# Hybrid decoder layer on one core: convolution taps tied to the weight splits and spread over more panels, block copies shared by two engines, and a reordered last norm

## The chip, the core and the metric

The kernel runs on one core of a Trainium2 chip. Four engines matter here: TensorE (PE, the matmuls; PEld is its weight load), VectorE (DVE), ScalarE (ACT) and GpSimd (POOL); SyncE (SP) issues the DMAs. The metric is the device time of one execution in microseconds, as the median of several runs.

## The reference

One layer, float32, for 256 tokens (x) and 256 memory tokens (mem), both 4096 wide:

```
proj = x @ w_in[l]                                  # 4096 x 11280
(c_a, c_b, c_gate, g_q, g_k, g_v, g_lr, g_gate, m_q, m_gate) = split(proj)
y_conv = _conv_group(c_a, c_b, dw, dw_b, ln_g, ln_b) * silu(c_gate)   # c_a * sigmoid(c_b), 31 taps per channel, norm, silu
y_gla  = _gla_group(g_q, g_k, g_v, g_lr, ...) * silu(g_gate)          # gated linear attention in chunks of 64
y_mem  = _memory_group(m_q, mem @ w_mem_kv[l]) * silu(m_gate)         # 4 heads of attention into the memory
out = concatenate([y_conv, y_gla, y_mem]) @ w_out[l]
x = _layernorm(DN_ALPHA * x + out, ln_g[l], ln_b[l])
```

## The kernel before

**Products.** Each float32 operand is split in two: ScalarE casts it to a rounded `hi` (L122), VectorE subtracts to get `lo` (L123), both in the helper `halves`. A product is then three matmuls, hi by hi, hi by lo and lo by hi. Weights are the moving side (128x512), x the stationary one. The work runs panel by panel (512 output columns) in the order of `STEPS`. A weight chunk is loaded by SP into one of three `raww` buffers; its halves go to four `hiw` and four `low` buffers (`WBUFS`), so the splitting can run ahead of PE by a few tiles and no more.

**Pairs.** Most panels are done two at a time in `pair` (sixteen chunks of 256 rows by 1024 columns). A chunk takes either eight block products (24 matmuls, two weight tiles "b" and "a") or seven (21 matmuls, four weight tiles "c", "a", "y" and "x"). For the seven, VectorE first makes sums of weight blocks: `tx` (L439) and `ty` in two steps (L445, L448), which ScalarE and VectorE then split like weights. The x side needs sums too (`sums`, tiles r, f, eh, el). `BY7` holds for each pair the pattern of eights and sevens, the x units whose chunks go by seven, the units whose sums are made before it, and those freed behind it. `X_AT` says at which chunk of the first pair each x unit is loaded.

**The order of stages.** Pair cb0 (columns c_b and c_a, first half), pair cb1 (second half), `memory` (mem by w_mem_kv, 64 tiles), pair mq, panels q0 and q1, pair k, panels v0 to v4, pairs gg0, gg2 and cg, panels mg0 and mg1, then the output projection: pairs o0, o1, o2 and two single panels.

**Work beside the matmuls.** Everything else (gates, attention, convolution, norms) is queued as closures and issued in between by the `use` function of each tile: `later` (end of a pair), `work` (in portions), and `fill` (convolution taps). A tap (L828, L837) is one VectorE operation on 128 channels; there are 31 for each of eight channel blocks, 248 in all, four blocks behind cb0 and four behind cb1. `FILLS` and `MEM_FILLS` say how many are taken from `fill` at a time. `queue_transpose` turns a 128x1024 tile: one VectorE transposition of 32x32 blocks (L229), then sixteen copies of 32x256 blocks on ScalarE (L243), four to each call of `moves`. It is used 22 times.

**Who sets the order.** The order on each engine is fixed when the program is built: a scheduler takes the instructions of the closures and arranges them, and may pull one ahead of others on its engine. `tc.issue_after(i)` keeps what stands under it behind instruction i. Each engine's queue is the order that the sections below print.

**The end.** The last panel (block 7) is finished token half by token half (tt 0, then tt 1). `norm_stats` makes mean and factor of a half, with a power on GpSimd (L1208); `norm_rows` brings the factors into a row layout by PE; `norm_apply` finishes the other blocks, on VectorE (L1264) or, with `on_pool`, on ScalarE (L1260, L1261) and GpSimd (L1262).

Of the kernel before, what the change touches and what calls it, by code (L numbers as in the profile page):

```python
# [9 lines left out]
F32 = mybir.dt.float32  # L10
# [18 lines left out]
EARLY = 5  # L29
AHEAD = 3  # L30

X_AT = {0: (1,), 1: (2,), 3: (3,), 4: (6,), 5: (4,), 6: (7,), 7: (5,)}

C_A, C_B, C_G, G_Q, G_K, G_V, G_LR, G_G, M_Q, M_G = 0, 1024, 2048, 3072, 4096, 5120, 7168, 7184, 9232, 10256

# [13 lines left out]

BY7 = {  # L50
    ("cb", 0): ("8888888887878787", (6, 7), (), ()),
    ("cb", 1): ("8888878787878787", (5, 6, 7), (5,), (5,)),
    ("mq", 0): ("8888888887878787", (6, 7), (), (6, 7)),
    ("k", 0): ("8888878787878787", (5, 6, 7), (5, 6, 7), (5,)),
    ("gg", 0): ("8888878787878787", (5, 6, 7), (5,), ()),
    ("gg", 2): ("8888878787878787", (5, 6, 7), (), (5,)),
    ("cg", 0): ("8887888788878887", (6, 7), (), (6, 7)),
}

FILLS = {("cb", 1): 1}  # L60
MEM_FILLS = 5


@with_exitstack
def layer_kernel(ctx, tc, xT, memT, xres, w_mem, w_in, w_pairs, w_last, cst, w_gate,
# [54 lines left out]
    def halves(src, hi, lo):  # L120

        nc.scalar.copy(out=hi, in_=src)  # L122
        nc.vector.tensor_tensor(out=lo, in0=src, in1=hi.bitcast(F32), op=ALU.subtract)  # L123

    def w_raw(shape, name):
        serial[0] += 1
# [94 lines left out]
    def queue_transpose(src, dst, then, back=False):  # L221


        st = {}

        def blocks():
            t = tmp.tile([P, 1024], F32, tag="T", name=f"T_{serial[0]}", bufs=1)
            serial[0] += 1
            nc.vector.transpose(out=t, in_=src.rearrange("p a b -> p (a b)"))  # L229
            give(src)  # L230
            st["t"] = t

        def moves(b):
            if b == 0:
                st["d"] = dst()
            tok = "p t (q j c) -> p t q j c"
            feat = "p q (t i c) -> p t q i c"
            flat = "p (q t i c) -> p t q i c" if back else "p (t q j c) -> p t q j c"
            sizes = dict(q=4, t=2, c=32)
            frm = st["t"].rearrange(flat, **sizes)  # L240
            to = st["d"].rearrange(tok if back else feat, c=32, **({"q": 4} if back else {"t": 2}))
            for a in range(4):
                nc.scalar.copy(  # L243
                    out=to[32 * b : 32 * b + 32, :, :, a, :],
                    in_=frm[32 * a : 32 * a + 32, :, :, b, :],
                )

        work.append(blocks)
        for b in range(4):
            work.append(lambda b=b: moves(b))  # L250
        work.append(lambda: then(st["d"]))
# [43 lines left out]
    def flush():  # L295
        while stream:
            stream.popleft()()


    def panel(chunks, width, stat, then, fills=0, apart=0, soon=KT // 2):  # L300

        banks = []
        held = {}
        raw = {}

        def mms(c, tt, w, second):
            for k in range(2):
                kt = 2 * c + k  # L310
                sh, sl = stat(kt // 4)
                for s in (sh,) if second else (sh, sl):
                    nc.tensor.matmul(  # L313
                        banks[tt][:, :width],
                        lhsT=s[:, kt % 4, tt * P : (tt + 1) * P],
                        rhs=w[:, k, :],
                        start=kt == 0 and not second and s is sh,
                        stop=kt == KT - 1 and second,
                    )

        def make(c):
            if c % 2 == 0:
                raw[0] = w_raw([P, 4, width], "w")
                nc.sync.dma_start(
                    out=raw[0], in_=chunks[c // 2].rearrange("p (k n) -> p k n", k=4)
                )
            w = w_tiles([P, 2, width], "w", KT // 2 - apart <= c < KT // 2 - WBUFS)
            halves(raw[0][:, 2 * (c % 2) : 2 * (c % 2) + 2, :], *w)
            held[c] = w

        def use(c):
            if c == 0:
                for tt in range(2):
                    serial[0] += 1
                    banks.append(acc.tile([P, 512], F32, tag="acc", name=f"acc_{serial[0]}"))
            if c < KT // 2 - apart:
                for w in held[c]:
                    for tt in range(2):
                        mms(c, tt, w, w is held[c][1])
            if later:  # L340
                later.popleft()()
            do_work(-(-len(work) // max(1, soon - c)))
            for _ in range(min(fills, len(fill))):
                fill.popleft()()

        for c in range(KT // 2):
            push(lambda c=c: make(c), lambda c=c: use(c))
        after(lambda: then(banks))

        def rest(k, tt):  # L350
            c = KT // 2 - apart + k
            for w in held[c]:
                mms(c, tt, w, w is held[c][1])

        return rest
# [13 lines left out]
    def pair(chunks, order, stat, ext, then, soon=KT // 2, fills=0, units=False, beside=None):  # L369
# [41 lines left out]
        def make(n, i):  # L411
            c, by7, tiles = plan[n]
            if i == 0:
                raw = w_raw([P, 4, 512], "w")
                ap = chunks[c].rearrange("p (k n) -> p k n", k=4)
                if beside and n == 0:

                    x0 = unit_tiles("x")
                    hi, lo = w_tiles([P, 2, 512], "w")
                    for k in range(2):  # L420
                        load(x0, four(xT[0]), k, k + 1)
                        load((raw[:, 2:4, :], hi, lo), ap[:, 2:4, :], 1 - k, 2 - k)
                    st[n, "b"] = hi, lo
                    nc.sync.dma_start(out=raw[:, 0:2, :], in_=ap[:, 0:2, :])
                    x_units[0] = load(x0, four(xT[0]), 2, 4)
                    give(x0[0])
                else:
                    nc.sync.dma_start(out=raw, in_=ap)
                if beside:
                    beside(n)  # L430
                src = st[n] = dict(a=raw[:, 0:2, :], b=raw[:, 2:4, :], c=raw[:, 2:3, :])
                if by7:
                    serial[0] += 1
                    if units:
# [13 lines left out]
                    nc.vector.tensor_tensor(  # L448
                        out=y[:, 1, :], in0=raw[:, 1, :], in1=y[:, 0, :], op=ALU.subtract
                    )  # L450
                    src.update(x=x, y=y)
            nm = tiles[i][0]
            if (n, nm) in st:
                return
            w = tuple(t[:, : 1 if nm == "c" else 2, :] for t in w_tiles([P, 2, 512], "w"))
            halves(st[n][nm], *w)
            st[n, nm] = w
            if i == len(tiles) - 1:
                src = st.pop(n)
                if by7 and units:  # L460
                    give(src["x"], src["y"])

        def use(n, i):
# [10 lines left out]
            for second in range(2):  # L474
                for j, (slot, stationary, bk) in enumerate(terms):
                    sh, sl = stationary(c)
                    for s in (sh,) if second else (sh, sl):
# [4 lines left out]
                            start=first[bk] == (n, nm, j) and not second and s is sh,  # L482
                            stop=last[bk] == (n, nm, j) and second == 1,
                        )
            if later:
                later.popleft()()
            if i == len(tiles) - 1:
                for _ in range(min(fills, len(fill))):
                    fill.popleft()()
                do_work(-(-len(work) // max(1, soon - n)))  # L490

        for n, (_, _, tiles) in enumerate(plan):
            for i in range(len(tiles)):
# [542 lines left out]
    def memory():  # L1036
        m_units, raws, tiles, banks = [], {}, {}, []

        def make(kt, half):
# [6 lines left out]
            if half == 1 and kt % 4 == 1 and kt < KT - 4:  # L1046
                m_units.append(load_unit("mem", four(memT[kt // 4 + 1])))
            tiles[kt, half] = w_tiles([P, 1024], "wm")
            halves(raw, *tiles[kt, half])

        def use(kt, half):
            while later and half == 1:
# [20 lines left out]
                            )  # L1073
            if half and kt % 4 == 3:
                give(mh, ml)
            if later:
                later.popleft()()
            do_work(-(-len(work) // max(1, KT - kt)))
            for _ in range(min(MEM_FILLS, len(fill))):
                fill.popleft()()  # L1080

        def done():
            mk.extend(unit([P, 2, 512], F32, "mk") for _ in range(2))
# [106 lines left out]
    z = []  # L1190
# [10 lines left out]
    def norm_stats(tt, g, beta):  # L1201
# [9 lines left out]
        nc.vector.tensor_scalar(  # L1211
            out=mn, in0=m[:, 0:1], scalar1=-1.0, scalar2=None, op0=ALU.mult
        )
        y = z[7][:, tt, :]
        nc.vector.scalar_tensor_tensor(
            out=y, in0=y, scalar=m[:, 0:1], in1=g, op0=ALU.subtract, op1=ALU.mult
        )
        c = cc[tt]
        nc.vector.tensor_scalar(
            out=c[:, 0:65:64], in0=mn.to_broadcast([P, 2]), scalar1=r, scalar2=None, op0=ALU.mult  # L1220
# [6 lines left out]
            op0=ALU.mult,  # L1227
            op1=ALU.subtract,
        )
        with tc.issue_after(cl.ins):  # L1230
            nc.vector.scalar_tensor_tensor(
                out=y, in0=y, scalar=r, in1=beta, op0=ALU.mult, op1=ALU.add
            )
# [165 lines left out]
    with tc.issue_after(last.ins):  # L1399
# [5 lines left out]
        with tc.issue_after(pw.ins):  # L1405
            norm_apply(0, (6,), on_pool=True)
        norm_rows(1)
        norm_apply(1, range(7))


def make_consts(nc, cpool, cst, norm_g):
# [91 lines left out]
```

## Time and profile before

| | |
|---|---|
| median of 3 runs | 1538.81 us (1537.97 to 1539.09) |
| profiled execution, its own time | 1540.91 us |
| its span in the profile | 1538.9 us |
| PE busy | 1506.4 us, 98%, 6809 matmuls |
| DVE busy | 1210.9 us, 79% |
| ACT busy | 901.6 us, 59% |
| POOL busy | 49.2 us, 3% |
| mean granted clock of TensorE | 0.993 of full speed |

The span runs from the first to the last instruction; the profiled execution's own time is 2.0 us longer, and 2.1 us above the median. A busy PE is not yet a PE at its peak, so how much a stage lost is told by its matmuls' count against its length. The page names the engine that ended each idle time.

### The profile page before, as it was taken

The numbers are of one execution on the slowest core, as the hardware profiler recorded it, in microseconds if no ns is written. First come the engines' busy times: TensorE is split into PE (matmuls) and PEld (weight loads), VectorE is DVE, ScalarE is ACT, GpSimd is POOL, SyncE is SP. The second block draws the span as 40 slices with busy tenths as digits, with TensorE's granted clock in tenths as the row PEclk, the third lists the DMA queues.
The fourth block names the chain that finished last, engine by engine and source line by source line (L and its number), as shares of the span: only waits on it lengthen the run. The fifth ranks groups of instructions, "written<-read, shape, count | busy, mean of one in ns | idle before, by whom it ended". The sixth has DMA issues, their size and how long they took to land.

```text
span 1538.9 us, 18500 instructions
## 1 busy us (share of the span) xinstructions
PE 1506.4 (98%) x6809; PEld 1265.8 (82%) x6809; DVE 1210.9 (79%) x1454; ACT 901.6 (59%) x1203; POOL 49.2 (3%) x59
## 2 busy tenths in 40 slices
PE   8999899999999999999999999999999999999997
PEld 6787678888888888899999887888888887888885
DVE  7799999997686579957575788887757589998955
ACT  6565357438668855676464468577685454555541
POOL 0000000000000000003030000000000000000001
PEclk9999999999999999999999999999999999999998
DMA  8564557765555465555445454656567545565662
GB/s 326 204 219 154 182 172 252 244 206 213 207 189 179 144 238 187 201 197 176 161 156 198 174 213 164 219 218 233 212 219 274 205 178 205 209 216 203 225 223 109
DMA packets 54515, 311.73 MB, mean 203 GB/s; under 512 B 6100, under 2 KB 6484, under 8 KB 27928
## 3 DMA queue, kind: packets, MB, share of 16 engines
q1 hardware_dynamic: 54424, 310.55, 57.1%
q8 instruction: 53, 0.87, 0.2%
q14 instruction: 38, 0.31, 0.1%
HBM read 304.24 MB, written 6.29 MB: 202 GB/s over the span
## 4 chain that ended last, share of the span: by engine, by line
PE 86%; DVE 6%; ACT 3%; issue 3%; DMA 2%; POOL 0%; SPq 0%; DVEq 0%; ACTq 0%
PE acc L478 29%; PE acc L313 28%; PE sm L478 8%; PE acc_N L478 8%; PE mv L1067 6%; PE mk L1067 6%; DVE low L123 2%; DVE cacc L837 2%; ACT S L243 1%; DMA rawx<-xT 1%; DMA raww<-w_in 1%; ACT hiw L122 1%; ACT qkT L243 1%; PE A L749 1%; PE o L274 1%
## 5 line engine op out<-in xcount | busy, mean ns | idle before, releaser
L123 DVE TENSOR_TENSOR low<-raww,hiw 128x1024 fp32r<-128x1024 f32 (+3 forms) x497 | 560.2, 1144 | 171.4 <-ACT hiw L122 139.6
L122 ACT CAST hiw<-raww 128x1024 fp32r<-128x1024 f32 (+3 forms) x497 | 476.7, 978 | 312.9 <-PE acc L313 125.6
L478 PE MATMUL acc<-hiw,hx 128*128 128x512 f32 x528 | 207.7, 393 | 6.1 <-ACT hiw L122 6.1
L313 PE MATMUL acc<-hiw,hx 128*128 128x512 f32 (+2 forms) x576 | 211.8, 368 | 0.1
L313 PE MATMUL acc<-hiw,lx 128*128 128x512 f32 (+2 forms) x576 | 211.7, 368 | 0.0
L478 PE MATMUL acc<-hiw,lx 128*128 128x512 f32 x528 | 206.7, 392 | 0.0
L478 PE MATMUL acc<-low,hx 128*128 128x512 f32 x528 | 169.0, 391 | 6.6 <-DVE low L123 6.6
L313 PE MATMUL acc<-low,hx 128*128 128x512 f32 (+2 forms) x576 | 141.7, 366 | 0.0
L122 ACT CAST hiw<-ty 128x1024 fp32r<-128x1024 f32 x52 | 54.6, 1050 | 130.4 <-DVE ty L448 93.0
L478 PEld LDWEIGHTS acc<-hiw,hx 128*128 128x128 f32 x528 | 100.0, 189 | 29.0 <-ACT hiw L122 8.2
L478 PEld LDWEIGHTS acc<-low,hx 128*128 128x128 f32 x528 | 99.1, 188 | 29.6 <-DVE low L123 9.3
L313 PEld LDWEIGHTS acc<-hiw,hx 128*128 128x128 f32 x576 | 108.2, 188 | 10.9 <-ACT hiw L122 0.4
L478 PEld LDWEIGHTS acc<-hiw,lx 128*128 128x128 f32 x528 | 100.0, 189 | 20.7
L313 PEld LDWEIGHTS acc<-hiw,lx 128*128 128x128 f32 x576 | 108.2, 188 | 10.3
L313 PEld LDWEIGHTS acc<-low,hx 128*128 128x128 f32 x576 | 107.2, 188 | 10.7
L122 ACT CAST hiwm<-rawwm 128x1024 fp32r<-128x1024 f32 x64 | 66.4, 1053 | 73.3 <-PE mv L1067 26.5
L837 DVE SCALAR_TENSOR_TENSOR cacc<-hT,cst_sb,cacc 128x255 f32<-128x255 f32 (+29 forms) x240 | 99.1, 462 | 0.0
L243 ACT COPY S<-T 32x256 f32<-32x256 f32 x224 | 90.3, 403 | 7.0 <-DVE T L229 3.2
L478 PE MATMUL acc<-hiw,xh 128*128 128x512 f32 x224 | 87.4, 390 | 1.6 <-ACT hiw L122 1.6
L123 DVE TENSOR_TENSOR low<-ty,hiw 128x1024 fp32r<-128x1024 f32 x52 | 63.6, 1222 | 31.7 <-ACT hiw L122 21.0
L478 PE MATMUL acc<-hiw,xl 128*128 128x512 f32 x224 | 87.2, 389 | 0.0
L439 DVE TENSOR_TENSOR tx<-raww 128x1024 f32<-128x1024 f32 x52 | 63.4, 1220 | 21.9 <-DMA raww<-w_in 21.8
(268 smaller groups left out, 2529.6 us busy)
## 6 DMA issues: line engine op xcount, KB each, us to landing
raww<-w_in SPq DMA_DIRECT2D x143, 1024.0 KB
raww<-w_pairs SPq DMA_DIRECT2D x48, 1024.0 KB
rawwm<-w_mem SPq DMA_DIRECT2D x64, 512.0 KB
raww<-w_in SPq DMA_DIRECT2D x32, 824.0 KB
raww<-w_last SPq DMA_DIRECT2D x16, 1024.0 KB
raww<-w_in SPq DMA_DIRECT2D x8, 832.0 KB
rawmem<-memT SPq DMA_DIRECT2D x8, 512.0 KB
xr<-xres SPq DMA_DIRECT2D x8, 512.0 KB
```

The lines of the kernel that those rows point to most:

```text
L122: nc.scalar.copy(out=hi, in_=src)
L123: nc.vector.tensor_tensor(out=lo, in0=src, in1=hi.bitcast(F32), op=ALU.subtract)
L243: nc.scalar.copy(out=to[32 * b : 32 * b + 32, :, :, a, :], in_=frm[32 * a : 32 * a + 32, :, :, b, :],)
L274: nc.tensor.matmul(ps, lhsT=a, rhs=b, start=t == 0 and k == 0, stop=t == n - 1 and k == 2)
L313: nc.tensor.matmul(banks[tt][:, :width], lhsT=s[:, kt % 4, tt * P : (tt + 1) * P], rhs=w[:, k, :], start=kt == 0 and not second and s is s ...
L439: nc.vector.tensor_tensor(out=x, in0=raw[:, 3:4, :].to_broadcast([P, 2, 512]), in1=raw[:, 0:3:2, :], op=ALU.subtract,)
L478: nc.tensor.matmul(bank_of(bk), lhsT=s, rhs=w[second][:, slot, :], start=first[bk] == (n, nm, j) and not second and s is sh, stop=last[bk] ...
L749: nc.tensor.matmul(ps[:, at : at + n], lhsT=keys[:, j, k0 : k0 + P], rhs=qs[:, j, q0 : q0 + n], start=dk == 0, stop=dk == 1,)
L837: nc.vector.scalar_tensor_tensor(out=a, in0=h, scalar=dw_sb[:, cb, j : j + 1], in1=a, op0=ALU.mult, op1=ALU.add)
L1067: nc.tensor.matmul(banks[half * 4 + a * 2 + mt], lhsT=s[:, kt % 4, mt * P : (mt + 1) * P], rhs=w[:, 512 * a : 512 * a + 512], start=kt == ...
```

## The change

1. `X_AT`: five of the seven x units that the first pair loads come one or two chunks later.
2. `BY7`: in pair mq two of the sixteen chunks go by seven, where four did; it needs the sums of unit 7 alone, and those of unit 6 are freed behind cb1.
3. `FILLS`, `MEM_FILLS`: two taps at a time in cb1 (one before), two in mq (three before), three in `memory` (five before).
4. `aside`: taps and portions of work now stand under `issue_after` of the newest `lo` that has been made (`made[0]`), taps first.
5. `moves`: of the sixteen copies behind a block transposition eight go to VectorE.
6. `norm_stats`: the first of block 7's two operations stands behind the factors, not ahead of them.
7. At the very end block 6 of the second token half goes to ScalarE and GpSimd, ahead of the other six.

```
-X_AT = {0: (1,), 1: (2,), 3: (3,), 4: (6,), 5: (4,), 6: (7,), 7: (5,)}
+X_AT = {0: (1,), 2: (2,), 4: (3,), 5: (6,), 6: (4,), 7: (7,), 9: (5,)}
...
-    ("cb", 1): ("8888878787878787", (5, 6, 7), (5,), (5,)),
-    ("mq", 0): ("8888888887878787", (6, 7), (), (6, 7)),
+    ("cb", 1): ("8888878787878787", (5, 6, 7), (5,), (5, 6)),
+    ("mq", 0): ("8888888788888887", (7,), (), (7,)),
...
-FILLS = {("cb", 1): 1}
-MEM_FILLS = 5
+FILLS = {("cb", 1): 2, ("mq", 0): 2}
+MEM_FILLS = 3
...
             for a in range(4):
-                nc.scalar.copy(
+                f = nc.scalar.copy if a % 2 else nc.vector.tensor_copy
+                f(
                     out=to[32 * b : 32 * b + 32, :, :, a, :],
...
+    made = [None]
+
+    def aside(n, taps):
+        if later:
+            later.popleft()()
+        with tc.issue_after(made[0].ins):
+            for _ in range(min(taps, len(fill))):
+                fill.popleft()()
+            do_work(n)
...
-            halves(raw[0][:, 2 * (c % 2) : 2 * (c % 2) + 2, :], *w)
+            made[0] = halves(raw[0][:, 2 * (c % 2) : 2 * (c % 2) + 2, :], *w)
...
-            if later:
-                later.popleft()()
-            do_work(-(-len(work) // max(1, soon - c)))
-            for _ in range(min(fills, len(fill))):
-                fill.popleft()()
+            aside(-(-len(work) // max(1, soon - c)), fills)
...
-        y = z[7][:, tt, :]
-        nc.vector.scalar_tensor_tensor(
-            out=y, in0=y, scalar=m[:, 0:1], in1=g, op0=ALU.subtract, op1=ALU.mult
-        )
...
+        y = z[7][:, tt, :]
         with tc.issue_after(cl.ins):
+            nc.vector.scalar_tensor_tensor(
+                out=y, in0=y, scalar=m[:, 0:1], in1=g, op0=ALU.subtract, op1=ALU.mult
+            )
...
         norm_rows(1)
-        norm_apply(1, range(7))
+        norm_apply(1, (6,), on_pool=True)
+        norm_apply(1, range(6))
```

What the scheduler makes of it shows in the engines' queues. VectorE in pair cb1, around the third chunk by seven; `cacc` rows are taps, `low` rows the remainders that PE waits for. Before:

```order
L445 TENSOR_TENSOR ty_1135<-raww_1132,tx_1134 128x512
L123 TENSOR_TENSOR low_1113<-raww_1110,hiw_1112 128x1024
L837 SCALAR_TENSOR_TENSOR cacc_1022<-hT_930,cst_sb,cacc_1022 128x249
L837 SCALAR_TENSOR_TENSOR cacc_1022<-hT_930,cst_sb,cacc_1022 128x248
L123 TENSOR_TENSOR low_1123<-raww_1110,hiw_1122 128x1024
L837 SCALAR_TENSOR_TENSOR cacc_1022<-hT_930,cst_sb,cacc_1022 128x248 x2
L448 TENSOR_TENSOR ty_1135<-raww_1132,ty_1135 128x512
L123 TENSOR_TENSOR low_1140<-raww_1132,hiw_1139 128x512
L837 SCALAR_TENSOR_TENSOR cacc_1022<-hT_930,cst_sb,cacc_1022 128x248
L837 SCALAR_TENSOR_TENSOR cacc_1022<-hT_930,cst_sb,cacc_1022 128x247
L123 TENSOR_TENSOR low_1151<-raww_1132,hiw_1150 128x1024
L837 SCALAR_TENSOR_TENSOR cacc_1022<-hT_930,cst_sb,cacc_1022 128x247 x3
```

And now, the same chunk (its buffers are numbered two higher):

```order
L454 TENSOR_TENSOR ty_1137<-raww_1134,tx_1136 128x512
L123 TENSOR_TENSOR low_1125<-raww_1112,hiw_1124 128x1024
L123 TENSOR_TENSOR low_1142<-raww_1134,hiw_1141 128x512
L842 SCALAR_TENSOR_TENSOR cacc_1022<-hT_969,cst_sb,cacc_1022 128x252
L457 TENSOR_TENSOR ty_1137<-raww_1134,ty_1137 128x512
L842 SCALAR_TENSOR_TENSOR cacc_1022<-hT_969,cst_sb,cacc_1022 128x251
L123 TENSOR_TENSOR low_1154<-raww_1134,hiw_1153 128x1024
L123 TENSOR_TENSOR low_1170<-ty_1137,hiw_1169 128x1024
```

Nine taps stood in the first piece, two stand in the second. Over the whole of pair cb1 the queue held 82 taps and holds 19; `memory` held 166 and holds 173, pair mq held none and holds 51, panel q0 holds the last 5. Pair cb1 also takes over from cb0 one making of x sums (r, four f, el), and one `lmem` from `memory`, and has eight `hT` copies.

ScalarE in pair gg2, around the second block transposition (`S` copies) of the two that open it; `hiw<-tx` is the last weight tile of the first chunk by seven. Before:

```order
L122 CAST xh_7702<-S_7681 128x1024
L122 CAST hiw_7663<-ty_7627 128x1024
L243 COPY S_7708<-T_7706 32x2x4x32 x13
L122 CAST hiw_7686<-tx_7626 128x1024
L243 COPY S_7708<-T_7706 32x2x4x32 x3
L122 CAST hiw_7734<-raww_7732 128x1024
```

And now:

```order
L122 CAST hiw_7643<-ty_7606 128x1024
L122 CAST xh_7682<-S_7665 128x1024
L122 CAST hiw_7659<-tx_7605 128x1024
L122 CAST hiw_7714<-raww_7712 128x1024
L122 CAST hiw_7725<-raww_7712 128x1024
L244 COPY S_7688<-T_7686 32x2x4x32 x8
```

The thirteen copies that stood ahead of `hiw<-tx` are gone from there; eight stand two weight tiles later, and the other eight are on VectorE.

VectorE at the very end, from the second half's factor `zrs` on. Before:

```order
L1211 TENSOR_SCALAR zmn_12071<-zmv_12066 128x1
L1215 SCALAR_TENSOR_TENSOR xr_11423<-xr_11423,zmv_12066,row_11950 128x512
L1219 TENSOR_SCALAR cc_9417<-zmn_12071,zrs_12068 128x2
L1222 SCALAR_TENSOR_TENSOR cc_9417<-zmn_12071,zrs_12068,cc_9417 128x1
L1231 SCALAR_TENSOR_TENSOR xr_11423<-xr_11423,zrs_12068,row_11952 128x512
```

And now:

```order
L1212 TENSOR_SCALAR zmn_12051<-zmv_12046 128x1
L1216 TENSOR_SCALAR cc_9397<-zmn_12051,zrs_12048 128x2
L1219 SCALAR_TENSOR_TENSOR cc_9397<-zmn_12051,zrs_12048,cc_9397 128x1
L1229 SCALAR_TENSOR_TENSOR xr_11403<-xr_11403,zmv_12046,row_11930 128x512
L1232 SCALAR_TENSOR_TENSOR xr_11403<-xr_11403,zrs_12048,row_11932 128x512
```

The first of block 7's two operations (`xr<-xr,zmv,row`), ahead of the factors `cc` before, stands behind them now. Behind these rows come seven L1264 operations before, and six (L1265) now.

## Rows read from the trace of the kernel before

**Rows 1.** The page of the kernel before, section 1 (busy time, share of the span, instructions of each engine) and section 4 (the chain of work that ended last, share of the span by engine).

```profile
PE 1506.4 (98%) x6809; PEld 1265.8 (82%) x6809; DVE 1210.9 (79%) x1454; ACT 901.6 (59%) x1203; POOL 49.2 (3%) x59
...
PE 86%; DVE 6%; ACT 3%; issue 3%; DMA 2%; POOL 0%; SPq 0%; DVEq 0%; ACTq 0%
```

**Rows 2.** Busy time by stage. Columns: the stretch, its length in us, busy us (and instructions) of PE, PEld, DVE, ACT and POOL, the granted clock of TensorE, the share of the DMA engines' time, GB/s. In order: pair cb0, pair cb1, `memory`, pair mq, panel q0, pair k, pair gg2.

```profile
5.80:97.00 91.20, 87.73 (x372) 71.74 (x373) 75.85 (x82) 53.84 (x58) 0.00 (x0) 1.00 0.70 258
97.00:199.50 102.50, 91.22 (x367) 70.08 (x366) 99.42 (x156) 54.30 (x69) 0.00 (x0) 0.95 0.53 180
199.50:375.10 175.60, 174.67 (x769) 143.98 (x768) 165.98 (x270) 98.40 (x129) 1.97 (x2) 1.00 0.64 212
375.10:459.50 84.40, 84.40 (x374) 69.86 (x374) 60.55 (x61) 57.32 (x82) 0.00 (x0) 1.00 0.59 214
459.50:508.80 49.30, 49.30 (x241) 41.75 (x240) 31.33 (x36) 41.22 (x77) 0.00 (x0) 1.00 0.51 173
556.70:641.10 84.40, 84.40 (x381) 70.16 (x380) 74.25 (x85) 52.33 (x67) 0.96 (x1) 1.00 0.53 187
923.10:1010.50 87.40, 85.16 (x367) 69.43 (x366) 74.33 (x77) 62.46 (x86) 0.00 (x0) 0.98 0.55 199
```

**Rows 3.** Waits that ended between 97 and 200 us, pair cb1: who waits <- for whom: us in total, times, longest.

```profile
ACT hiw L122 <- DVE ty L448: 20.9, 5, 6.9
...
PE acc L478 <- ACT hiw L122: 5.7, 3, 2.5
PE acc L478 <- DVE low L123: 4.9, 6, 1.6
```

**Rows 4.** Pair cb1 again, first DVE alone from 118 us on, then the taps (L837) alone, in cb1 and in `memory`: length, DVE busy us (and instructions), clock, DMA share, GB/s.

```profile
118.00:199.50 81.50, 81.50 (x135) 0.94 0.52 175
97.00:199.50 102.50, 33.39 (x79) 0.95 0.53 180
199.50:375.10 175.60, 65.75 (x162) 1.00 0.64 212
```

**Rows 5.** The sequence on DVE at two places, in pair cb1 and in pair gg2: start, length, engine, line, operation, count.

```profile
131.40 1.26 DVE L837 SCALAR_TENSOR_TENSOR cacc<-hT,cst_sb,cacc 128x252 f32<-128x252 f32 x3
132.57 1.22 DVE L123 TENSOR_TENSOR low<-raww,hiw 128x1024 fp32r<-128x1024 f32 x1
133.71 0.68 DVE L445 TENSOR_TENSOR ty<-raww,tx 128x512 f32<-128x512 f32 x1
134.31 0.47 DVE L837 SCALAR_TENSOR_TENSOR cacc<-hT,cst_sb,cacc 128x252 f32<-128x252 f32 x1
...
940.95 0.68 DVE L445 TENSOR_TENSOR ty<-raww,tx 128x512 f32<-128x512 f32 x1
941.66 0.69 DVE L448 TENSOR_TENSOR ty<-raww,ty 128x512 f32<-128x512 f32 x1
```

**Rows 6.** Groups by line and shape: line, engine, operation, count, busy us, mean ns of one, idle time ahead of them and what ended most of it; the last row is from the view of line 828 alone and has the shortest, median and longest ns.

```profile
L190 DVE TENSOR_TENSOR f<-r 128x256 f32<-128x256 f32 x20 | 7.5, 416 | 3.2 <-ACT qkT L243 3.2
L243 ACT COPY S<-T 32x256 f32<-32x256 f32 x224 | 90.3, 403 | 7.0 <-DVE T L229 3.2 <-DVE xl L123 1.3
...
L828 DVE TENSOR_SCALAR cacc<-hT,cst_sb x8: 408/408/412, 118.0 to 241.2; 128x256 f32<-128x256 f32 x8
```

**Rows 7.** Two short stretches with a lowered clock, in pair cb1 and in pair gg2, columns as in the second group.

```profile
165.20:172.10 6.90, 5.28 (x13) 4.13 (x14) 6.90 (x12) 4.82 (x6) 0.00 (x0) 0.51 0.44 152
957.00:960.50 3.50, 3.44 (x9) 2.22 (x8) 3.09 (x5) 3.48 (x5) 0.00 (x0) 0.52 0.00 0
```

**Rows 8.** Pair gg2, around one stop of PE, on ACT, DVE and PE (start, length, engine, line, operation, count, [idle time before it <- what ended it]).

```profile
949.57 5.39 ACT L243 COPY S<-T 32x256 f32<-32x256 f32 x13 [0.66 <-DVE xl L123]
954.98 1.04 ACT L122 CAST hiw<-tx 128x1024 fp32r<-128x1024 f32 x1
956.06 1.23 DVE L123 TENSOR_TENSOR low<-tx,hiw 128x1024 fp32r<-128x1024 f32 x1 [4.25 <-ACT hiw L122]
953.51 0.39 PE L478 MATMUL sm<-low,eh 128*128 128x512 f32 x1
956.08 0.50 PE L478 MATMUL sm<-hiw,eh 128*128 128x512 f32 x1 [2.18 <-ACT hiw L122]
```

**Rows 9.** Pair cb0, on ACT and on DVE, as above.

```profile
25.40 2.00 ACT L122 CAST hiw<-raww 128x1024 fp32r<-128x1024 f32 x2 [1.53 <-DVE f L190]
...
62.06 1.23 DVE L439 TENSOR_TENSOR tx<-raww 128x1024 f32<-128x1024 f32 x1 [5.79 <-DMA raww<-w_in]
```

**Rows 10.** The end of the program, on DVE, POOL and PE, as above.

```profile
1518.03 0.23 DVE L1219 TENSOR_SCALAR cc<-zmn,zrs 128x2 fp32r<-128x2 f32 x1 [0.44 <-POOL zrs L1208]
...
1526.76 0.74 DVE L1215 SCALAR_TENSOR_TENSOR xr<-xr,zmv,row 128x512 f32<-128x512 f32 x1
1526.93 0.98 POOL L1208 TENSOR_TENSOR zrs<-zrs,negh 128x1 f32<-128x1 f32 x1
...
1527.88 1.25 POOL L1262 TENSOR_TENSOR xr<-xr,w 128x512 f32<-128x512 f32 x1
1527.94 1.22 DVE L1219 TENSOR_SCALAR cc<-zmn,zrs 128x2 fp32r<-128x2 f32 x1 [0.44 <-POOL zrs L1208]
...
1530.30 3.75 PE L1254 MATMUL mg<-gb,ccT 128*128 128x512 f32 x7 [0.35 <-ACT ccT L1246]
1531.13 4.70 DVE L1264 SCALAR_TENSOR_TENSOR xr<-xr,zrs,mg 128x512 f32<-128x512 f32 x7 [1.06 <-PE mg L1254]
```

More of the change, by code (lines that the diff above doesn't have):

```diff
@@ L122, in halves @@
         nc.scalar.copy(out=hi, in_=src)
-        nc.vector.tensor_tensor(out=lo, in0=src, in1=hi.bitcast(F32), op=ALU.subtract)
+        return nc.vector.tensor_tensor(out=lo, in0=src, in1=hi.bitcast(F32), op=ALU.subtract)
     def w_raw(shape, name):
@@ L455, in make @@
             w = tuple(t[:, : 1 if nm == "c" else 2, :] for t in w_tiles([P, 2, 512], "w"))
-            halves(st[n][nm], *w)
+            made[0] = halves(st[n][nm], *w)
             st[n, nm] = w
@@ L484, in use @@
                         )
[L485 to L490, printed above, removed]
+            done = i == len(tiles) - 1
+            aside(-(-len(work) // max(1, soon - n)) if done else 0, fills if done else 0)
         for n, (_, _, tiles) in enumerate(plan):
@@ L1048, in make @@
             tiles[kt, half] = w_tiles([P, 1024], "wm")
-            halves(raw, *tiles[kt, half])
+            made[0] = halves(raw, *tiles[kt, half])
         def use(kt, half):
@@ L1075, in use @@
                 give(mh, ml)
[L1076 to L1080, printed above, removed]
+            aside(-(-len(work) // max(1, KT - kt)), MEM_FILLS)
         def done():
```

## The prediction, made before the changed kernel ran

> **What bounds the kernel now.** I read the page first. TensorE is busy 98% of the span, and the chain that ended last lies on it for 86% [rows 1]. So time can only be won where PE stops or runs slowly, and the next view is the busy time by stage. A 512-column matmul that waits for nothing starts every 0.227 us: pair mq does its 372 in 84.4 us and its DVE has 24 us to spare [rows 2]. Held against this, 372 matmuls (84.4 us) fill 91.2 us in cb0 (6.8 lost), 366 (83.1) fill 102.5 in cb1 (19.4 lost), 768 (174.3) fill 175.6 in `memory` (1.3 lost), 366 fill 87.4 in gg2 (4.3 lost); mq, q0 and k lose nothing.
>
> Pair cb1 is therefore the place. The reader is to see there that VectorE works 99.42 of 102.5 us, and from 118 us on without a gap, 81.50 of 81.50 [rows 2, 4]; 33.39 us of it are taps, which no matmul of this pair needs [rows 4]. The waits say how they hurt: ScalarE's `hiw` waits 20.9 us for `ty`, up to 6.9 at once, and PE then waits for `hiw` or `low` [rows 3]. PE's clock drops behind the longer waits: 0.51 of full speed, the lower level, from 165.2 to 172.1, while DVE is full [rows 7].
>
> **Prices.** Operations that follow each other on DVE overlap. Three taps at 131.40 let the next start 1.17 later: 0.39 each. A 1024-wide `low` lasts 1.22 and the next starts after 1.14 (0.08 sooner than its end); a 512-wide one takes 0.60 of the queue [rows 5]. A dependent pair starts 0.71 apart instead of 0.60, 0.11 more [rows 5].
>
> The new 32x256 copies on DVE are not in the trace; on ScalarE one takes 0.403 [rows 6]. Nearest rows on DVE: 256 elements last 0.416 with two inputs and 0.408 with one [rows 6], so about 0.33 of the queue with the usual overlap. Bounds: 0.20 if a copy ran at half the 512-to-1024 slope (0.54/2 for 512, 0.13 for 256, and a fixed 0.06); 0.45 if each waited for the one ahead to end, as the dependent pair does. I take 0.33, as the one-input row is no cheaper than the two-input one.
>
> The Trainium skill (VectorE: DVE Perf Modes, "The perf-mode tier table") lists float32 copies from SBUF at twice the rate of two-input operations, together with tensor_scalar. Its figures for 2048 elements would give an estimate of some 0.29 for 256. The trace disagrees in so far as the one-input 0.408 shows no doubling; by the page the eight copies of a transposition would cost 0.3 us less.
>
> **The change, step by step.**
>
> *cb1.* Taps go from 82 to 19: 63 x 0.39 = -24.6 us of DVE. Added: one making of x sums (r 1.14, four f 4 x 0.34, el 1.14 = +3.6), one `lmem` +1.1, eight copies 8 x 0.33 = +2.6; one `cb` less, -0.6. Together -17.9. DVE sets the length, so 102.5 - 17.9 = 84.6, still 1.5 above PE's 83.1. **-17.9.** Bounds: -19.4 if PE alone is left; -12.4 if 7 us stay, because the copies come eight in a row among sevens. The tile buffers let PE be at most three tiles behind the split: in sevens 3 x 21/4 x 0.227 = 3.6 us, in eights 8.2. Around the first chunk by seven the new queue holds (sums, `lmem`, lows) some 11.9 us of DVE against 4.8 of PE; without more lead than 3.6 this alone is 3.5 us, and a clock drop as at 165.2 doubles it.
>
> *`memory`.* 7 more taps, +2.7 us on 166 of DVE in 175.6, so PE stays the bound; the taps now stand behind the newest `low` and not ahead of it. **-0.8** of the 1.3 (bounds -1.3 to +1).
>
> *mq and q0.* Two sevens become eights: six matmuls, 6 x 0.227 = +1.4, on PE for certain. DVE: 51 taps +19.9, 16 copies +5.3, two sevens fewer -8.2 (each has tx, two ty, and four lows in place of two: 6.4 against 2.3): 60.6 becomes 77.6 of 85.8. That work lies beside PE's; without the cover it would cost up to its 19.9. I allow +0.3 (0 to 2). **+1.7.** In q0 the last five taps, a transposition and the norm behind it find 18 us free [rows 2]: 0.
>
> *k.* Fourteen copies, one r and one xl: +6.9, 74.3 becomes 81.2 of 84.4 [rows 2]. That is tight, so **+1.0** (0 to 4).
>
> *gg2.* ScalarE does thirteen copies, 5.39 us, ahead of `hiw<-tx`; `low<-tx` follows at 956.06, and PE sits from 953.51 to 956.08 [rows 8]; then the clock is at 0.52 for 3.5 us [rows 7]. In the new order no copies stand there. Late next is DVE: 74.3 + 16 x 0.33 = 79.6 of 83.1, with about 25 us of it in three chunks of 15 us of PE. I take half: **-2.2** (-4.3 to 0). The other transpositions gain nothing: their ScalarE copies are hidden.
>
> *End.* DVE's last row of seven takes 4.70, 0.67 each [rows 10]. Six take 4.03, but begin one `mg` later: 512 columns at the lower level of 1.2 GHz, 0.43. **-0.2.** The moved first operation of block 7 was hidden behind POOL's power (1526.76 to 1527.91); now it runs behind `cc`, done at about 1530.8, before the first DVE row can start: nothing. Cc's L1219 took 1.22 beside POOL's addition and 0.23 without it [rows 10]; POOL's new addition now runs beside DVE's six, so bounds -0.7 to +1.0.
>
> *cb0.* Its two larger stops wait for DMAs: the casts at 25.40 directly behind x and weights, and `tx` at 62.06, 5.79 us for its weights [rows 9]. An x unit later on SP's queue lets weights past, and itself comes later. 0 (-3.8 to +2.3).
>
> Sum: -17.9 - 0.8 + 1.7 + 1.0 - 2.2 - 0.2 = -18.4. From the profiled execution's 1540.9 this is 1522.5; it stood 2.1 above the median, so **1520.4 us**.
>
> **Rivals.**
>
> 1. *Dear copies and bursts* (0.20). Each copy costs 0.45: cb1's DVE gets 1 us more, k's 1.7 (82.9 of 84.4), and eight copies take 3.6 us, all the lead that sevens have. Then the upper bounds hold: cb1 -12.4, `memory` 0, mq +3.4, k +4, gg2 0, end 0: -5.0, 1533.8; half way between, 1527. For it: no DVE copy with a partition offset is in the trace. Against: k absorbs 74 of 84 us without any loss. The Trainium skill (VectorE: DVE Perf Modes, "Two Vector instructions with no wait between them") says that an instruction waits for all earlier ones when its input or output starts in another quarter of the partitions than the last one's. These copies change quarters each time, so by that rule the overlap is gone. The dependent pair's 0.11 is the only row near it, and bears another cause.
> 2. *More than cb1 is freed* (0.10). cb1 becomes PE-bound (-1.5 more), gg2 loses its whole stop (-2.1), cb0's two stops shrink (-3.8): 1513.
> 3. *No gain* (0.03). The flood only moves: the 19.4 us come back in mq and k. That needs DVE full there; mq, q0 and k have 24 + 18 + 10 us free, and the added work is 17 + 7 + a few.
> 4. *Slower* (0.05). On DVE a transposition's eight copies hold up the lows behind them. There are 22 transpositions; if each stops PE for s us, the gain of 18.4 is gone from s = 0.84. At s = 2 (gg2's stop was 2.2, before the clock's share) the time is 1520.4 + 44 = 1564. Against it: 8 x 0.33 = 2.6 us is less than either lead, 3.6 or 8.2; it decides only if copies cost 0.55 or more.
>
> **The numbers.** The likeliest case (0.62) has its own range of 1515 to 1526. The range for 8 in 10 adds most of rival 1 and the upper part of rival 2: 1513.5 to 1531. A change of under 0.2%, 3 us, can't be told from none here. Faster: 0.62 + 0.20 + 0.10, as even rival 1's upper bound of 1533.8 is 5 us below; same 0.03; slower 0.05.
>
> **What would show it.** cb1 should last 84 to 86 us with DVE no longer full, and no wait for `ty` of more than 3 us; taps should appear in mq (51) with PE still back to back, 85.8 long. One DVE copy should take 0.30 to 0.45. In gg2 the stop at `hiw<-tx` should be gone. The last row of DVE should hold six operations. The prediction is wrong if cb1 stays over 92 us, if k or mq lose over 4, or if PE waits for `low` behind copies at many transpositions.

## The result, and the profile after

The changed kernel takes 1523.35 us (median of 4 runs, 1522.33 to 1525.94) where the kernel before takes 1538.95 (1537.97 to 1540.05): a ratio of 0.9901, interval 0.9884 to 0.9918, so 15.6 us faster. Its profiled execution took 1522.78, its span is 1521.0, 17.9 under the span before.

The page after, sections 1 and 4 (compare [rows 1]):

```profile
PE 1499.4 (99%) x6815; PEld 1265.4 (83%) x6815; DVE 1258.0 (83%) x1619; ACT 835.4 (55%) x1025; POOL 49.7 (3%) x60
...
PE 95%; DVE 2%; DMA 2%; ACT 0%; issue 0%; SPq 0%; POOL 0%; DVEq 0%; ACTq 0%
```

PE's share of the chain went from 86% to 95%. DVE is 47 us busier, ScalarE 66 less: 176 copies changed engine.

Busy time by stage, after, columns as in [rows 2]; in order cb0, cb1, `memory`, mq, q0, q1, k, gg2:

```profile
5.30:94.40 89.10, 86.96 (x373) 70.86 (x374) 74.08 (x78) 54.25 (x58) 0.00 (x0) 0.98 0.72 266
94.40:178.80 84.40, 83.23 (x367) 68.50 (x366) 81.28 (x106) 51.03 (x60) 0.00 (x0) 1.00 0.64 217
178.80:353.10 174.30, 174.30 (x769) 144.06 (x768) 170.18 (x288) 83.71 (x93) 0.00 (x0) 1.00 0.65 215
353.10:438.80 85.70, 85.70 (x380) 70.96 (x379) 72.78 (x107) 47.28 (x61) 0.00 (x0) 1.00 0.54 185
438.80:485.20 46.40, 46.40 (x217) 38.90 (x216) 45.70 (x77) 33.73 (x51) 1.97 (x2) 1.00 0.68 249
485.20:534.60 49.40, 49.40 (x242) 41.78 (x241) 37.19 (x58) 33.17 (x60) 0.00 (x0) 1.00 0.51 171
534.60:622.90 88.30, 86.99 (x391) 71.22 (x390) 78.07 (x95) 48.80 (x60) 0.96 (x1) 1.00 0.53 184
904.60:993.90 89.30, 85.93 (x367) 70.33 (x366) 78.34 (x93) 56.08 (x70) 0.00 (x0) 0.96 0.55 195
```

Read the second line against [rows 2]: cb1 lasts 84.40 instead of 102.50, at full clock, DVE busy 81.28 instead of 99.42. `memory` and mq run without a gap. Twenty-four matmuls of the attention moved from q0 to q1 and k, twelve to each, so q0, q1 and k are compared together: 184.1 against 181.6 before. The last line is the surprise: gg2 is 1.9 us longer than before.

Waits that ended in cb1, after (compare [rows 3]):

```profile
ACT hiw L122 <- DVE ty L457: 4.8, 2, 3.8
...
PE acc L487 <- ACT hiw L122: 1.2, 1, 1.2
```

20.9 us of waits for `ty` became 4.8, and PE stops once.

The new stop in gg2, after: DVE, then ScalarE, then PE (columns as in [rows 8]).

```profile
926.85 2.36 DVE L244 COPY S<-T 32x256 f32<-32x256 f32 x8
929.24 1.23 DVE L123 TENSOR_TENSOR low<-raww,hiw 128x1024 fp32r<-128x1024 f32 x1
930.38 1.24 DVE L229 STREAM_TRANSPOSE T<-o 128x1024 f32<-128x1024 f32 x1
...
936.05 2.36 DVE L244 COPY S<-T 32x256 f32<-32x256 f32 x8
...
944.52 1.23 DVE L448 TENSOR_TENSOR tx<-raww 128x1024 f32<-128x1024 f32 x1 [0.25 <-DMA raww<-w_in]
945.66 0.69 DVE L457 TENSOR_TENSOR ty<-raww,ty 128x512 f32<-128x512 f32 x1
...
946.73 1.04 ACT L122 CAST hiw<-ty 128x1024 fp32r<-128x1024 f32 x1 [6.20 <-DVE ty L457]
...
947.83 0.80 PE L487 MATMUL acc<-hiw,hx 128*128 128x512 f32 x1 [3.37 <-ACT hiw L122]
```

The stop behind ScalarE's thirteen copies is gone [rows 8]. In its place DVE has work without a pause from 917 to 944: the two products with `gg`, both transpositions, sixteen copies, two `xl`, and the sums for the sevens among and behind all of it. `hiw<-ty` waits 6.20 us for `ty`, PE 3.37 for `hiw`, and behind that the clock is at 0.50 for 6.8 us:

```profile
946.20:953.00 6.80, 5.17 (x12) 4.11 (x13) 6.50 (x8) 5.45 (x6) 0.00 (x0) 0.50 0.42 155
```

In k, PE stops for a `low` that stands behind an x sum on DVE, and for an `eh` that ScalarE casts from a late one:

```profile
568.64 0.73 PE L487 MATMUL acc_N<-low,hx 128*128 128x512 f32 x2 [0.50 <-DVE low L123]
570.06 0.50 PE L487 MATMUL acc<-hiw,eh 128*128 128x512 f32 x1 [0.68 <-ACT eh L122]
```

The end, after (compare [rows 10]):

```profile
1509.20 0.55 POOL L1209 TENSOR_TENSOR zrs<-zrs,negh 128x1 f32<-128x1 f32 x1
...
1509.79 0.23 DVE L1216 TENSOR_SCALAR cc<-zmn,zrs 128x2 fp32r<-128x2 f32 x1 [0.67 <-POOL zrs L1209]
1509.90 1.26 POOL L1263 TENSOR_TENSOR xr<-xr,w 128x512 f32<-128x512 f32 x1 [0.15 <-ACT w L1262]
1510.05 1.13 DVE L1219 SCALAR_TENSOR_TENSOR cc<-zmn,zrs,cc 128x1 fp32r<-128x1 f32 x1
...
1513.32 4.04 DVE L1265 SCALAR_TENSOR_TENSOR xr<-xr,zrs,mg 128x512 f32<-128x512 f32 x6 [0.69 <-PE mg L1255]
1513.61 1.28 POOL L1263 TENSOR_TENSOR xr<-xr,w 128x512 f32<-128x512 f32 x1 [2.45 <-ACT w L1262]
```

Six operations take 4.04. POOL's power takes 0.55 instead of 0.98, now that no 128x512 operation of DVE runs beside it; the wait in `cc` behind POOL's addition is still there, 1.13 instead of 1.22, only one operation later. What is left of the span behind DVE's last row is the stores of `xr`. All of them, before and after (issue time in ns: shortest, median, longest; start of the first and of the last in us):

```profile
L1238 SPq DMA_DIRECT2D out<-xr x16: 332/332/383, 1519.2 to 1535.9; - x16
L1239 SPq DMA_DIRECT2D out<-xr x16: 332/333/473, 1501.8 to 1517.4; - x16
```

The last store is issued 3.0 us ahead of the end of the span before, and 3.6 after. So DVE's last row ends 0.7 sooner, counted from the first matmul of the last panel, but the span only 0.1 (59.6 and 59.5).

### The profile page after: what moved, and what is told of

Same layout as the page of the kernel before. It is cut to its first block, busy times and chain, and to the rows that moved or that the text cites. A ratio compares the mean times of both kernels' runs of the same rounds, so it can differ in the third digit from the quotient of the medians.

```text
span 1521.0 us, 18490 instructions
## 1 busy us (share of the span) xinstructions
PE 1499.4 (99%) x6815; PEld 1265.4 (83%) x6815; DVE 1258.0 (83%) x1619; ACT 835.4 (55%) x1025; POOL 49.7 (3%) x60
## 4 chain that ended last, share of the span: by engine, by line
PE 95%; DVE 2%; DMA 2%; ACT 0%; issue 0%; SPq 0%; POOL 0%; DVEq 0%; ACTq 0%
PE acc L487 34%; PE acc L326 29%; PE acc_N L487 9%; PE sm L487 9%; PE mk L1072 6%; PE mv L1072 6%; DMA raww<-w_in 2%; PE A L754 1%; DVE low L123 1%; PE o L275 1%; PE sc L275 0%; PE mo L275 0%; ACT hiw L122 0%; DVE xr L1265 0%; SPq L149 0%
## 5 line engine op out<-in xcount | busy, mean ns | idle before, releaser
L487 PEld LDWEIGHTS acc<-hiw,lx 128*128 128x128 f32 x536 | 101.1, 189 | 20.9
L842 DVE SCALAR_TENSOR_TENSOR cacc<-hT,cst_sb,cacc 128x239 f32<-128x239 f32 (+27 forms) x240 | 101.9, 463 | 0.6
L123 DVE TENSOR_TENSOR lowm<-rawwm,hiwm 128x1024 fp32r<-128x1024 f32 x64 | 77.7, 1220 | 2.5 <-ACT hiwm L122 1.5
L487 PE MATMUL acc<-low,xh 128*128 128x512 f32 x224 | 71.7, 389 | 0.2 <-DVE low L123 0.2
```

What stands on the lines that cost most here:

```text
L123: return nc.vector.tensor_tensor(out=lo, in0=src, in1=hi.bitcast(F32), op=ALU.subtract)
L487: nc.tensor.matmul(bank_of(bk), lhsT=s, rhs=w[second][:, slot, :], start=first[bk] == (n, nm, j) and not second and s is sh, stop=last[bk] ...
L842: nc.vector.scalar_tensor_tensor(out=a, in0=h, scalar=dw_sb[:, cb, j : j + 1], in1=a, op0=ALU.mult, op1=ALU.add)
```

## Experiments

Two theories stood against each other: the tied and spread taps carry the gain and the shared copies only move work (mine, from the prediction); or the shared copies carry a part of it. All runs are against the kernel before on the same chip.

**The changed kernel with all copies on ScalarE.**

```
-                f = nc.scalar.copy if a % 2 else nc.vector.tensor_copy
+                f = nc.scalar.copy
```

> The changed kernel with all sixteen copies of a block transposition on ScalarE again; taps, tail and x loads stay. Theory (the taps carry the gain, the shared copies only move work): pair cb1 stays at 84 to 86 us and k loses 0 to 1 us, where the changed kernel loses 2.5 in q1 and k; in gg2 DVE is 4.8 us emptier and the 3.5 us stop behind ty goes, but ScalarE's sixteen copies stand ahead of a hiw again, so 3 to 5 us are lost there. Time 0 to 4 us under the changed kernel's 1523.4, 1519 to 1523. Rival (sharing the copies is needed for the gain): stops behind ScalarE's copies appear at several transpositions, time 1526 to 1532.

1532.03 us, ratio 0.9954 (0.9940 to 0.9968): 8.7 over the changed kernel. The rival is right, my theory of the copies is not. gg2 is 2.3 shorter, as expected, but mq lasts 2.0 longer, q1 and k together 4.3, cg 4.4, cb1 and `memory` 2.6.

**The kernel before with the new taps alone.** The diff's `aside`, `FILLS`, `MEM_FILLS` and `BY7`, nothing else.

> The kernel before with the new taps alone: tie, counts for cb1, memory and mq, and mq's two sevens fewer; x loads, copies and tail are those of before. Theory: cb1 85 us (-17.5), memory -1.3, mq +1.4, everything else as before: 1538.9 - 17.4 = 1521.5, range 1519 to 1524. Rival (the copies carry part of it): cb1 at 88 us or more, since its first transposition's copies are on ScalarE, time 1526 or more.

1532.28 us, ratio 0.9964 (0.9950 to 0.9978). The stretches, in order cb1, mq, q1, k:

```profile
94.40:180.40 86.00, 83.66 (x368) 68.40 (x366) 80.27 (x99) 54.99 (x69) 0.00 (x0) 1.00 0.62 209
354.80:442.50 87.70, 85.99 (x380) 70.89 (x379) 66.56 (x87) 52.98 (x77) 0.00 (x0) 1.00 0.53 182
488.90:541.30 52.40, 50.11 (x241) 41.35 (x239) 25.69 (x32) 43.24 (x90) 0.00 (x0) 1.00 0.51 179
541.30:630.90 89.60, 87.50 (x391) 71.07 (x391) 80.05 (x91) 55.77 (x73) 0.96 (x1) 1.00 0.53 188
```

cb1 is at 86.0, near the 85 that I said: the taps alone empty it. But the time is 8 above my range: 8.8 us are given back in mq, q0, q1 and k, where PE did not stop once before, and 1.8 in cg. What stops PE in mq, on ScalarE, DVE and PE:

```profile
394.48 6.62 ACT L244 COPY S<-T 32x256 f32<-32x256 f32 x16
401.12 3.90 ACT L122 CAST hiw<-raww 128x1024 fp32r<-128x1024 f32 x4
...
402.20 2.36 DVE L123 TENSOR_TENSOR low<-raww,hiw 128x1024 fp32r<-128x1024 f32 x2 [5.81 <-ACT hiw L122]
...
402.22 0.50 PE L487 MATMUL acc<-hiw,hx 128*128 128x512 f32 x1 [1.71 <-ACT hiw L122]
```

Sixteen copies now stand in one block on ScalarE, 6.62 us, ahead of a cast, and they use up the lead of the tiles.

**The changed kernel without the tie.**

```
-        with tc.issue_after(made[0].ins):
-            for _ in range(min(taps, len(fill))):
-                fill.popleft()()
-            do_work(n)
+        for _ in range(min(taps, len(fill))):
+            fill.popleft()()
+        do_work(n)
```

> The changed kernel without the tie of taps and work to the newest low; counts, mq's pattern, copies and tail stay. The queue then holds 77 taps in cb1 and none in mq, although two at a time are allowed in mq and three in memory. Theory (what counts is how many taps stand in cb1's DVE queue, and the tie alone puts them elsewhere): cb1 is DVE-bound again, 58 taps more than in the changed kernel, 58 x 0.39 = 22.6 us less what the changed order had to spare (3): cb1 102 to 106 us, time 1538 to 1546. Rival (the counts and the pattern do it, or it is the place of a tap behind its low and not the number): cb1 under 95 us, time under 1533.

1537.06 us, ratio 0.9990 (0.9981 to 0.9999). cb1 and gg2:

```profile
94.00:193.90 99.90, 88.50 (x368) 70.81 (x367) 99.31 (x157) 50.97 (x59) 0.00 (x0) 0.95 0.53 180
921.50:1005.40 83.90, 83.50 (x367) 68.46 (x366) 77.86 (x93) 55.15 (x70) 0.00 (x0) 1.00 0.58 208
```

The counts alone do nothing: without the tie 77 taps are in cb1's queue and DVE is full again. 99.9 is 2 under my range, since without the tie the making of x sums (r, four f, el: 3.5 us of DVE) does not stand in cb1 either. And gg2 is whole: 83.9. Its new stop belongs to the tie, too.

**The kernel before with the copies shared.**

> The kernel before with eight of the sixteen copies of every block transposition on VectorE and nothing else. Theory: in cb1 four taps fewer (78) and eight copies more stand in the queue, 8 x 0.30 - 4 x 0.39 = +0.8 us; in gg2 the stop moves from ScalarE's thirteen copies to VectorE, loss 4 to 7 us where before lost 4.3; k loses 0 to 3 us. Time 1538 to 1544, nothing gained. Rival (ScalarE's copies were what made hiw late in cb1 and gg2): 2 to 6 us faster, 1533 to 1537.

1532.36 us, ratio 0.9960 (0.9947 to 0.9972), 6.5 faster where I expected nothing. cb1 and gg2:

```profile
94.50:193.20 98.70, 89.19 (x367) 71.33 (x366) 98.06 (x157) 50.21 (x59) 0.00 (x0) 0.93 0.54 180
917.60:1000.60 83.00, 83.00 (x367) 68.63 (x366) 77.82 (x93) 54.93 (x70) 0.00 (x0) 1.00 0.57 206
```

gg2's stop goes altogether. In cb1 the copies end DVE's own wait for its first transposition, 2.74 us before, and four taps leave; against its own 102.5 (103.4 in a second profile, below) it gains 4 to 5. The row of before:

```profile
117.95 1.38 DVE L828 TENSOR_SCALAR cacc<-hT,cst_sb 128x256 f32<-128x256 f32 x4 [2.74 <-ACT hT L243]
```

**The tie split.** This left a new theory: the tie does two things. Kept on the taps it empties cb1; kept on the portions of work (`do_work`) it delays the transpositions, which then fall as one block among the casts and sums of later chunks. The shared copies halve that block.

```
         with tc.issue_after(made[0].ins):
             for _ in range(min(taps, len(fill))):
                 fill.popleft()()
-            do_work(n)
+        do_work(n)
```

> The changed kernel with the tie for the taps only; the portions of work are queued without it. Theory (the tie does two things: it keeps taps out of cb1, worth some 15 us, and it delays the portions of work, whose transpositions then fall among chunks by seven and stop PE): cb1 stays near 84.5 us with 19 taps, k loses 0 to 0.5 instead of 2.5 us, gg2 0 to 1.5 instead of 6.3, as in the runs without any tie. Time 1523.4 - 2.5 - 5.3 = 1515.6, range 1513.5 to 1518. Rival (the stops in k and gg2 come from the copies on VectorE themselves, or from the taps in mq): they stay, time 1521 to 1525.

1516.48 us (1515.47 to 1520.00), ratio 0.9858 (0.9845 to 0.9872): 6.9 under the changed kernel, 22.4 under the kernel before, the best of all. cb1, mq, k and gg2:

```profile
94.90:179.40 84.50, 83.41 (x368) 68.35 (x367) 79.16 (x101) 51.42 (x60) 0.00 (x0) 1.00 0.63 219
353.60:439.30 85.70, 85.70 (x379) 70.95 (x379) 72.63 (x107) 47.29 (x61) 0.00 (x0) 1.00 0.54 186
...
536.50:620.90 84.40, 84.40 (x380) 70.14 (x379) 76.34 (x93) 50.02 (x58) 0.96 (x1) 1.00 0.54 187
902.60:986.40 83.80, 83.40 (x368) 68.47 (x367) 77.89 (x93) 55.20 (x70) 0.00 (x0) 1.00 0.56 208
```

k has its 84.4 back and gg2 is at 83.8, with the same copies on DVE and the same taps in mq. So the rival (copies or taps as the cause of these stops) is out.

**The same with all copies on ScalarE.**

> The same (tie for the taps only), with all sixteen copies on ScalarE. Theory (the copies on VectorE mainly mend what the delayed work breaks; without the delay they are worth only gg2's stop): gg2 loses 4 to 4.5 as in the kernel before, cg 1.2, mq, q1 and k 0 to 0.5, cb1 1.5 to 3: 1515.6 + 4 + 1 + 0.7 = 1521, range 1518 to 1523. Rival (sharing is worth about 9 us by itself, as between the changed kernel and the one with all copies on ScalarE): 1524 to 1527.

1528.19 us, ratio 0.9931 (0.9918 to 0.9943). My figure was 7 too low: sharing is worth 11.7 us even without the delay. gg2's stop is there as expected (86.4), cg loses 3.7, and q1 is 5.1 longer than with shared copies, which I had not seen:

```profile
507.45 4.97 ACT L244 COPY qkT<-T 32x256 f32<-32x256 f32 x12
512.44 1.04 ACT L122 CAST hiw<-raww 128x1024 fp32r<-128x1024 f32 x1
...
513.54 0.50 PE L326 MATMUL acc<-hiw,hx 128*128 128x512 f32 x1 [2.28 <-ACT hiw L122]
```

Twelve copies in one block once more, here of q's transposition. Sixteen copies of another transposition (from 496.14, 6.63 us) stand close ahead of them, with two weight casts between the blocks; in the kernel before, four such casts stand between its blocks of sixteen at 470.60 and 482.00. Behind the stop the clock is lowered: from 515.1 to 517.7 the matmuls start 0.43 apart. Why the copies stand in a block in this order and not in the one before (q1 lost nothing there) is not settled; what they cost is.

**The tie on the work alone.** The reverse split: the taps are queued outside the tie, `do_work` inside.

> The changed kernel with the tie for the portions of work only; the taps are queued without it. The queue then holds 64 taps in cb1 and none in mq. Theory: cb1 loses 9 to 17 us (64 - 19 = 45 taps more, 17.5 us, of which 1.5 to 3 were to spare), k 2 to 4 and gg2 5 to 7 as in the changed kernel: time 1534 to 1544. Rival (the tie of work carries the gain in cb1): cb1 under 90 us, time under 1528.

1537.30 us, ratio 0.9989 (0.9979 to 0.9998). 64 taps are in cb1, which lasts 97.4; k (with q0 and q1) loses 2.5, as in the changed kernel, and gg2 4.8, where the changed kernel loses 6.2. Both halves of the theory hold.

**The old counts.** One tap at a time in cb1, five in `memory`, three in mq; the tie and the rest stay.

> The changed kernel with the old counts: one tap at a time in cb1, five in memory, three in mq, of which none are left there; the tie stays. The queue holds 10 taps in cb1, 238 in memory, none in mq. Theory (VectorE's work per stretch decides): memory has 65 taps more, 65 x 0.39 = 25 us on a VectorE that had 174.3 - 161 = 13 to spare, so it loses 10 to 14 us; cb1 0 to 1.5; mq 0. Time 1523.4 + 11 = 1534, range 1531 to 1538. Rival (the taps cost nothing anywhere as long as they stand behind their low): memory loses under 3 us, time 1520 to 1525.

1544.68 us, ratio 1.0037 (1.0023 to 1.0051), slower than before, and by 10 more than I expected. cb1 is without any loss (82.97 us), `memory` loses 25. Not a little at each tile: in one stop, on DVE and PE.

```profile
288.14 20.42 DVE L842 SCALAR_TENSOR_TENSOR cacc<-hT,cst_sb,cacc 128x242 f32<-128x242 f32 x54
...
309.64 1.18 DVE L123 TENSOR_TENSOR lmem<-rawmem,hmem 128x1024 fp32r<-128x1024 f32 x1
...
310.87 2.08 PE L1072 MATMUL mk<-hiwm,lmem 128*128 128x512 f32 x4 [22.28 <-DVE lmem L123]
```

54 taps stand in a row ahead of an `lmem`. The tie bounds a tap from one side only: it may not come before its `low`, but nothing keeps it from standing ahead of what PE wants next.

**The kernel before once more, and two small parts of the change.** One execution each: 1537.50, 1538.07 and 1538.70 us. Only their profiles are used: of cb0, of the end, and as a second profile of before.

> The kernel before, unchanged, for a second profile. In the first one cb0 lost 6.9 us, 2.3 of them behind a DMA at 62 us; in the changed kernel and in the kernel with only the copies shared, which does not touch cb0, it lost 4.6 to 4.7. Theory (the stop at 62 us is a late DMA of that one execution): cb0 loses 4 to 5.5 us now; cb1, gg2, cg, o1 and the end are as in the first profile within 0.5 us. Rival (the old order has it always): 6.5 us or more.

> The kernel before with the later x loads of the first pair alone. Theory (they are no term): cb0 loses 4 to 5.5 us, like the kernels with the old places; the rest as before, time 1536 to 1541. Rival (they free the weights' DMAs): cb0 under 3.5 us.

> The kernel before with the new end alone: block 7's first operation behind the factors, block 6 of the second half on ScalarE and GpSimd ahead of six on VectorE. Theory: from the last weight matmul to the end 0.5 to 1.0 us less, the last row of VectorE 4.03 instead of 4.70 and POOL's power shorter; the rest as before, 1536 to 1541. Rival (GpSimd's new addition slows VectorE's six): that row lasts over 4.6.

The second profile of before, cb0, cb1 and gg2:

```profile
5.30:94.70 89.40, 86.95 (x372) 70.85 (x373) 75.81 (x82) 53.77 (x58) 0.00 (x0) 0.98 0.71 265
94.70:198.10 103.40, 91.96 (x367) 71.57 (x366) 100.32 (x158) 55.19 (x69) 0.00 (x0) 0.94 0.53 179
...
920.90:1007.30 86.40, 83.83 (x367) 68.50 (x366) 73.89 (x77) 61.74 (x86) 0.00 (x0) 1.00 0.54 198
```

cb0 lasts 89.4, 1.8 less than in the first profile, with nothing changed: `tx` near 60 waits 3.69 us for its DMA, not 5.79. gg2 differs by 1.0, as its clock did not drop this time, and cb1 by 0.9; I had expected both within 0.5. With the later x loads alone (six of the seven units come later, not five as the list of the change says) cb0 lasts 90.0, between the two profiles of before: they are no term. With the new end alone DVE's last row, its six in 4.04, ends 0.9 sooner after the first matmul of the last panel (55.6 instead of 56.5); POOL's addition does not slow the six. But the span ends only 0.2 sooner (59.3 instead of 59.5), under the 0.5 to 1.0 that I expected: 3.7 us pass from the issue of the last store to the end, where 3.0 pass in the kernel before. Every run with the new end has 3.6 to 3.7 there and every run with the old one 3.0; why is not settled.

## Why the prediction held, point by point

1520.4 was forecast and 1523.35 measured, inside the own range of the likeliest case. The sum of the profile was nearer still, -18.4 against -17.9. But that holds against the first profile of before; against the second the span is 14.5 shorter, and the medians differ by 15.6. The forecast also carried over the 2.1 us by which the first profiled execution of before stood above the median, while the changed kernel's stood 0.6 below its own. Nor were the terms all right, and part of the agreement is two errors that cancel. The rows add up to the difference of the spans but for rounding.

| step | forecast | against the first profile | against the second |
|---|---|---|---|
| cb0 | 0 | -2.2 | -0.4 |
| cb1 | -17.9 | -18.0 | -18.9 |
| `memory` | -0.8 | -1.3 | -0.5 |
| mq, q0, q1, k | +2.7 | +3.9 | +3.9 |
| gg2 | -2.2 | +1.9 | +2.9 |
| end | -0.2 | -0.1 | -0.1 |
| v0, cg, o1, o2 | none | -1.5 | -1.4 |
| ahead of the first matmul | none | -0.4 | +0.1 |

- *cb1* held, with its mechanism and size: DVE was the bound, and taking 63 taps out moved the bound to PE. The split of the tie shows that the tie on the taps does it (84.5 with it alone, 97.4 with the tie on the work alone). DVE's busy time fell by 18.1 where 17.9 was summed, and the stretch came out as that account had it, 84.4 against 84.6.
- *The copies' price* came out lower than I took it: 283 ns each, and eight in 2.36 us, so 0.297 of the queue against 0.33.

```profile
L244 DVE COPY S<-T 32x256 f32<-32x256 f32 x112 | 31.7, 283 | 1.7
```

  A copy is much faster than the 0.408 of the one-input row [rows 6], on which I had built, and it does not overlap with its neighbour: each starts 0.014 after the one ahead ended, and the `low` behind them 0.03 after. The Trainium skill (VectorE: DVE Perf Modes, "The perf-mode tier table") has float32 copies at twice the rate, worked out as an estimate of 0.29, and the trace agrees. The rule of the same page of the Trainium skill in "Two Vector instructions with no wait between them" (no overlap when the quarter of the partitions changes) agrees as well with the missing overlap. In the price of 0.33 the shorter copy and the missing overlap cancelled to within 0.04 us. The first rival's condition, 0.45 each, was not met. (Its sum is also too low: it says that the upper bounds hold, but takes `memory` and the end at 0 where their upper bounds were +1 each, which would give 1535.8.)
- *mq* came out as forecast, +1.4 for the two eights and no stop, but with DVE at 72.8 and not 77.6: of the 51 taps that the queue gives to it some ten ran while PE was still in `memory`. No run keeps the old pattern of mq with the new taps, so whether the two eights are worth their 1.4 us is open.
- *gg2* failed, in sign and outside its bounds. The step said that without the thirteen copies half of the stop would go; DVE's overload there (79.6 of 83.1, 25 us against 15 in three chunks) was seen, but not that the tied order moves both transpositions closer to the sums of the first sevens. The cause is the tie on the work: without it gg2 lasts 83.8.
- *k* was sized at +1.0, and with q0 and q1 costs 2.5, inside its bounds; it has the same cause.
- *"The other transpositions gain nothing: their ScalarE copies are hidden"* failed. In the order before they were hidden but for cb1's first, for which DVE waited 2.74 us. In the tied order they are not, and sharing them is worth 8.7 us, which the forecast took for nothing. It came out in the sum all the same, since I had not charged the tie for what it breaks in mq, q1, k and cg. The two errors cancel: this is luck, not insight.
- *cb0*: the fall is mostly the difference of two executions of the same code.
- *End*: DVE's last row gained 0.7 and not 0.2, but the longer wait for the last store, which was no term, took most of it back, so that the -0.2 came out near the measured -0.1 by luck. "Hidden behind POOL's power" was wrong for the moved operation of block 7: it lengthened the power by 0.43 (0.98 against 0.55).

The rivals: more than cb1 freed and no gain did not come; the one that is slower neither, though its mechanism, copies in a block ahead of `low` or `hiw`, is what costs in gg2, and on ScalarE in the versions that don't share them.

## What to carry to other kernels

A tie that holds side work back has to be costed for everything that stands under it: here the tie on the taps is worth 20.6 us (1537.06 without any tie, 1516.48 with this one), and the tie on the portions of work beside them costs 6.9. In a queue that is in order, the length of the longest block of side work ahead of an urgent instruction counts, against the lead of the buffers, and not the engine's share of busy time: q1 lost 5 us with ScalarE busy 47 of 56. Before a term of a few us is booked from one profile, a second profile of the same kernel tells whether it is there at all.

## What the hardware showed beside that

A 32x256 float32 copy from SBUF to SBUF takes 283 ns on VectorE and 403 on ScalarE. GpSimd's 128x1 power took 0.98 us beside a 128x512 operation on VectorE, and 0.55 without; a 128x1 operation on VectorE that starts during a 128x512 addition on GpSimd took 1.13 to 1.22 instead of 0.22, until that addition was over, but VectorE's six 128x512 operations, which read `mg`, lasted no longer beside it (4.04, 0.67 each, as in the row of seven before).
